# A different order of DMAs, additions, weight pieces and parameter steps in a kernel's opening

## The chip, the cores and the metric

One core of one Trainium2 chip runs the kernel, which is a single launch. The metric is the device time of one execution in microseconds (us). The kernel before takes 1205.55 us, the median of 3 runs from 1204.6 to 1206.71.

## What is computed

512 tokens (256 context tokens, then 256 latent ones) of width 1024 pass through two layers. The part of the reference that the opening of layer 0 computes, and the mixers whose preparation runs beside it:

```python
x = x + _pos_embed_2d(...)                    # latent tokens only: row part, column part
sh1, sc1, ... = split(silu(c) @ w_mod + b_mod) # c_ctx for the context tokens
h = x * rsqrt(mean(x * x) + EPS) * g * (1 + sc1) + sh1
z = h @ w_in                  # 5 * 256 mixer columns, 4 * 1024 gate columns
dt = exp(log_dt); mag = exp(lam_re * dt); ang = lam_im * dt      # S5 parameters
a_re, a_im = mag * cos(ang), mag * sin(ang)   # then f, b_bar, and a scan over the tokens
y = [s5(z0), fnet(z1), pool(z2), conv31(z3 * sigmoid(z4))]       # four branches
x = x + gate1 * ((sum of sigmoid(z_gate) * (y @ w_branch)) @ w_out)
```

## The kernel before

The activations lie transposed, with features on the partitions: `X[:, k, :]` is feature tile k (of 8) of all 512 tokens. A float32 product is made of three matmuls on a high and a low part of each factor (`tile_mm`, line 64 in the profile as for every recorded operation). The high and low parts of the normed input are `HH` and `HL`, in the tensor `parts`.

**Weights.** `Stream` brings 512 KB pieces in a fixed order on SyncE's (SP's) queue into three buffers. ScalarE (ACT) copies the high part, VectorE (DVE) subtracts it and so makes the low part: rows `TENSOR_TENSOR parts<-whole,parts 128x1024`, called a *low* below. `weight(j)` takes such a piece.

**Modulation.** `w_mod` comes in sixteen 512 KB pieces for the first half. `mod_part()` multiplies the next one (16 rows `bank<-..., 128*32 128x128` in the trace for a piece). Four pieces make one accumulated group, after which ACT copies it; `mod_finish(m)` then computes shift and scale of two feature tiles (m, m+1). `h_tiles` makes HH and HL of one tile per `next(h)`. `group(k, j)` is the three matmuls of feature tile k with weight j. In the opening, mod tiles 0 to 7 are wanted in pairs by the groups of k = 0 to 7. Four weights (j = 0 to 3) are multiplied in this way, 32 groups or 96 matmuls in all.

**Norm.** DVE and GpSimd (POOL) add the position tables to the latent half of X, ACT squares each tile, DVE adds the eight squares, and one set of four matmuls sums over features; `norm_steps` makes 1/rms of it.

**Warm matmuls.** `warm(n)` issues n products of 128x256 whose result nothing reads; there are 18 in the opening (7, then 2, 2, 0, 1, 2, 4).

**Background tasks.** The S5 parameters are computed by generators: `S5.prep` (small DVE operations, then complex powers), `tables_b` (48 DVE operations 128x256 that make 16 tables), `tables_c` (the same for the readout, on POOL, after a DMA from `s5c` at line 325), then a scan. `step(task, n)` advances one by n yields; in the opening it is called 3 times with 3, and once with 1. After the opening a planner (`pump`) puts the steps of all tasks between the matmuls by estimated engine times, so that a changed opening changes the order of everything that follows it in layer 0.

**After the opening** come the products of the weights in an order given by a string: z tiles 6, 8, 7, 9, then gate tiles (`g20`...), branch products (`q..`), and `y20`, `y10`: places where DVE splits a finished branch (FNet is y10) into high and low parts, which PE's next `q10` needs. In the trace these splits are rows `parts<-mixer,parts 128x512 x2`. The convolution needs z tile 9: its gate is a row `TENSOR_TENSOR scan<-scan,whole 128x512` (shown as 128x2x256 in the order rows); after it come 62 rows `SCALAR_TENSOR_TENSOR scan<-scan,whole 128x512`, two for each of 31 taps.

Of the kernel before, what the change touches and what calls it, by code (L numbers as in the profile page):

```python
# [104 lines left out]
class S5:  # L105
# [10 lines left out]
    def prep(self, tmp):  # L116
# [10 lines left out]
        K.nc.sync.dma_start(par, K.I["s5p"][self.l][:, 0:48])  # L127
        K.nc.sync.dma_start(raw, K.I["s5p"][self.l][:, 48:560])
# [608 lines left out]
class Model:  # L737
# [357 lines left out]
    def norm_steps(self, accs, n, width, d=None):  # L1095
# [3 lines left out]
        pss = [self.aux() for _ in accs]  # L1099
# [185 lines left out]
    def layer(self, l):  # L1285
# [10 lines left out]
        if l == 0:  # L1296
# [14 lines left out]
            parts(2)  # L1311
            self.warm(2)
            norm = self.norm_steps(((self.ACC,),), 512, 1024)
            next(norm)
            self.warm(2)
            parts(1)
            self.warm(0)
            parts(1)
            y = [y for y in norm][-1]
            self.warm(1)  # L1320
            self.mod_finish(0)
            self.warm(2)
# [5 lines left out]
            self.warm(4)  # L1328
            h = self.h_tiles(l, 0, r, 0, 512)
            weight(0)  # L1330
            next(h)
            next(h)
            group(0, 0)
            self.stream.advance(1)
            self.mod_ahead = 16
            parts(1)
            next(h)
            weight(1)
            parts(1)
            group(1, 0)  # L1340
            weight(2)
            parts(2)
            group(0, 1)
            self.mod_finish(2)
            next(h)
            next(h)
            group(1, 1)
            group(0, 2)
            group(1, 2)
            self.step(tab[0], 3)  # L1350
            group(2, 0, 1, 2)
            parts(1)
            weight(3)
            group(3, 0)
            parts(1)
            group(3, 1)
            parts(1)
            parts(1)
            group(3, 2)
            self.mod_finish(4)  # L1360
            next(h)
            next(h)
            group(0, 3)
            group(1, 3)
            group(2, 3)
            group(3, 3)
            self.step(tab[0], 3)
            group(4, 0, 1)
            parts(2)
            group(4, 2)  # L1370
            parts(2)
            group(4, 3)
            self.mod_finish(6)
            next(h)
            next(h)
            self.step(tab[0], 3)
            group(5, 0, 1, 2, 3)
            group(6, 0, 1, 2, 3)
            group(7, 0, 1, 2, 3)
        else:  # L1380
            gw = []

# [290 lines left out]
    def run(self):  # L1673
        nc = self.nc
# [462 lines left out]
```

## Time and profile before

| | us |
|---|---|
| median of 3 runs | 1205.55 |
| profiled execution, own time | 1209.18 |
| its span from first to last instruction | 1207.2 |
| PE busy in the span | 1160.9 (96%) |
| DVE busy | 976.1 (81%) |
| ACT busy | 517.1 (43%) |
| POOL busy | 282.9 (23%) |
| mean granted TensorE clock | 0.986 of full |

The profiled execution took 3.63 us more than the median, of which 1.98 us lie outside its span. A busy engine is one that holds an instruction; TensorE (PE) is busy nearly all of the time, so that time is to be had from its waits, from the stretches at a lower clock and from its work. Rows of the timeline give the start of a run of like instructions, its length, the engine, operation, tiles, shape and count, and in brackets the idle time ahead of it with what ended it. A start is counted from the span's start.

### The profile page before, as it was taken

The numbers are of one execution on the slowest core, as the hardware profiler recorded it, in microseconds if no ns is written. First come the engines' busy times: TensorE is split into PE (matmuls) and PEld (weight loads), VectorE is DVE, ScalarE is ACT, GpSimd is POOL, SyncE is SP. The second block draws the span as 40 slices with busy tenths as digits, with TensorE's granted clock in tenths as the row PEclk, the third lists the DMA queues.
The fourth block names the chain that finished last, engine by engine and source line by source line (L and its number), as shares of the span: only waits on it lengthen the run. The fifth ranks groups of instructions, "written<-read, shape, count | busy, mean of one in ns | idle before, by whom it ended". The sixth has DMA issues, their size and how long they took to land.

```text
span 1207.2 us, 20297 instructions
## 1 busy us (share of the span) xinstructions
PE 1160.9 (96%) x7770; PEld 1009.4 (84%) x7770; DVE 976.1 (81%) x1878; ACT 517.1 (43%) x872; POOL 282.9 (23%) x319
## 2 busy tenths in 40 slices
PE   7999897999999999999999899999899999999997
PEld 5777675777888988888887778898899999999997
DVE  6789989977999769999988883546998788867764
ACT  4534242344324365422332333346544556645543
POOL 0038656000000100166555561020520001000000
PEclk9999999999999999999999999999899999999999
DMA  9543531644674514466578774425554545555551
GB/s 366 225 144 109 180 92 52 229 156 138 212 229 156 173 37 148 140 188 230 186 245 296 249 247 180 130 98 177 173 166 167 159 160 205 177 190 179 189 182 48
DMA packets 66513, 211.49 MB, mean 175 GB/s; under 512 B 7984, under 2 KB 13616, under 8 KB 66416
## 3 DMA queue, kind: packets, MB, share of 16 engines
q1 hardware_dynamic: 55456, 183.84, 45.4%
q10 hardware_dynamic: 7696, 14.56, 3.3%
q0 software_dynamic: 3264, 11.80, 2.9%
q8 instruction: 61, 1.00, 0.3%
q14 instruction: 36, 0.29, 0.1%
HBM read 199.19 MB, written 10.98 MB: 174 GB/s over the span
## 4 chain that ended last, share of the span: by engine, by line
PE 72%; DVE 15%; POOL 3%; DMA 3%; issue 3%; ACT 3%; ACTq 0%; POOLq 0%; DVEq 0%; SPq 0%
PE bank L64 72%; DVE scan L64 5%; DVE parts L64 4%; DVE mixer L64 2%; DVE whole L64 2%; ACT parts L64 2%; POOL tables L64 1%; POOL whole L64 1%; ACT whole L64 1%; DVE windows L64 1%; POOL scan L64 1%; DMA whole<-in_w_in_dram 1%; DMA whole<-in_x_dram 0%; DMA scan<-scr_z 0%; DMA scr_c<-tables 0%
## 5 line engine op out<-in xcount | busy, mean ns | idle before, releaser
L64 PE MATMUL bank<-parts 128*128 128x512 f32 (+2 forms) x4008 | 727.2, 339 | 19.0 <-DVE parts L64 16.6
L64 PEld LDWEIGHTS bank<-parts 128*128 128x128 f32 x4008 | 616.3, 191 | 105.4 <-DVE parts L64 22.3
L64 ACT ACTIVATE parts<-whole 128x1024 fp32r<-128x1024 f32 (+1 forms) x288 | 273.7, 959 | 144.9 <-PE bank L64 73.9
L64 DVE TENSOR_TENSOR parts<-whole,parts 128x1024 fp32r<-128x1024 f32 (+1 forms) x240 | 294.0, 1233 | 16.0 <-ACT parts L64 15.6
L64 PE MATMUL bank<-hidden,parts 128*128 128x256 f32 (+1 forms) x1440 | 251.2, 335 | 0.0
L64 PEld LDWEIGHTS bank<-hidden,parts 128*128 128x128 f32 x1440 | 217.5, 188 | 29.9 <-issue 0.3
L64 DVE SCALAR_TENSOR_TENSOR whole<-whole 128x1024 f32<-128x1024 f32 (+4 forms) x188 | 175.7, 936 | 15.2 <-DMA whole<-in_w_modt_dram 12.0
L64 POOL TENSOR_TENSOR whole<-whole 128x256 f32<-128x256 f32 (+1 forms) x69 | 50.3, 743 | 347.2 <-ACT whole L64 342.2
L64 DVE SCALAR_TENSOR_TENSOR whole<-bank,whole 128x256 f32<-128x256 f32 (+1 forms) x121 | 54.7, 475 | 66.4 <-PE bank L64 66.2
L64 ACT ACTIVATE whole<-whole 128x256 f32<-128x256 f32 (+2 forms) x139 | 48.9, 388 | 107.2 <-DVE whole L64 96.4
L64 ACT ACTIVATE mixer<-bank 128x512 f32<-128x512 f32 (+1 forms) x84 | 40.7, 496 | 119.8 <-PE bank L64 110.3
L64 DVE TENSOR_TENSOR whole<-whole 128x256 f32<-128x256 f32 (+7 forms) x158 | 73.0, 467 | 16.7 <-ACT whole L64 11.7
L64 ACT ACTIVATE whole<-bank 128x512 f32<-128x512 f32 (+2 forms) x69 | 35.5, 537 | 109.1 <-PE bank L64 77.5
L64 POOL TENSOR_TENSOR tables<-tables,whole 128x256 f32<-128x256 f32 x48 | 61.4, 1287 | 37.4 <-DMA scr_c<-tables 34.9
L64 DVE TENSOR_TENSOR hidden<-whole,hidden 128x512 fp32r<-128x512 f32 (+2 forms) x77 | 53.4, 698 | 9.0 <-ACT hidden L64 2.4
L64 ACT ACTIVATE hidden<-whole 128x512 fp32r<-128x512 f32 (+2 forms) x77 | 47.1, 615 | 8.2 <-PE bank L64 2.3
L64 ACT ACTIVATE tables<-bank 128x512 f32<-128x512 f32 (+2 forms) x20 | 8.4, 422 | 92.8 <-PE bank L64 92.5
L64 POOL COPY whole<-whole 128x32 f32<-128x32 f32 x20 | 11.9, 626 | 150.3 <-DVE whole L64 150.3
L64 POOL TENSOR_TENSOR scan<-scan,whole 128x256 f32<-128x256 f32 (+3 forms) x50 | 44.0, 892 | 12.0 <-DVE scan L64 8.3
L64 DVE SCALAR_TENSOR_TENSOR scan<-scan,whole 128x512 f32<-128x512 f32 (+1 forms) x64 | 42.7, 728 | 0.0
L64 PE MATMUL bank<-merged,parts 128*128 128x256 f32 (+1 forms) x240 | 38.0, 316 | 0.8 <-DVE merged L64 0.8
L64 DVE TENSOR_TENSOR scan<-scan,whole 128x256 f32<-128x256 f32 (+5 forms) x61 | 31.5, 543 | 9.0 <-ACT whole L64 8.0
(115 smaller groups left out, 899.0 us busy)
## 6 DMA issues: line engine op xcount, KB each, us to landing
whole<-in_w_dram SPq DMA_DIRECT2D x128, 512.0 KB, 4.3
whole<-in_w_in_dram SPq DMA_DIRECT2D x84, 512.0 KB, 4.3
whole<-in_w_modt_dram SPq DMA_DIRECT2D x78, 512.0 KB, 4.1
whole<-in_w_br_dram SPq DMA_DIRECT2D x16, 512.0 KB, 4.4
whole<-in_w_out_dram SPq DMA_DIRECT2D x16, 512.0 KB, 4.2
mixer<-in_w_mod_dram SPq DMA_DIRECT2D x8, 512.0 KB, 9.7
scan<-scr_b POOLq DMA_DIRECT2D x8, 512.0 KB, 5.2
scan<-in_w_mod_dram SPq DMA_DIRECT2D x6, 512.0 KB, 9.7
```

The lines of the kernel that those rows point to most:

```text
L64: return f(out, *a, **k)
```

## The change

The S5 parameters' first load (48 columns) is issued first on SP's queue, ahead of X; the remaining 512 columns come after modulation piece 7, with a yield between the two. The first weight stands ahead of the modulation pieces. The two position tables become one DMA, first on ACT's queue, and DVE makes all eight additions. The squares are added in pairs on DVE, and PE sums the four pairs (16 matmuls of 128x1 in place of 4). Sigmoid runs after the first two squares and not before them. Thirteen of the 18 warm matmuls are gone. The steps of `prep` are called at 9 places (17 steps with the empty one) in place of 4 (10 steps). The groups and modulation pieces are multiplied in another order. The rows of `layer` that are taken out are in the listing above, and are shortened to a line of dots here.

```diff
--- before.py
+++ after.py
@@ -125,6 +125,7 @@
         par = A(48)
         raw = A(512)
         K.nc.sync.dma_start(par, K.I["s5p"][self.l][:, 0:48])
+        yield
         K.nc.sync.dma_start(raw, K.I["s5p"][self.l][:, 48:560])
         T = [A(16) for _ in range(12)]
         lr, li, dt = par[:, 0:16], par[:, 16:32], par[:, 32:48]
@@ -1092,11 +1093,11 @@
             self.nc.scalar.activation(t[:, sl], self.X[:, k, sl], AF.Square)
             self.defer(lambda: E.tensor_tensor(self.ACC[:, sl], self.ACC[:, sl], t[:, sl], op=ADD))
 
-    def norm_steps(self, accs, n, width, d=None):
+    def norm_steps(self, accs, n, width, d=None, pss=None):
         nc, V = self.nc, self.nc.vector
         self.settle()
         nt = n // 128
-        pss = [self.aux() for _ in accs]
+        pss = pss or [self.aux() for _ in accs]
         for ps, group in zip(pss, accs):
             for i in range(nt):
                 for a in group:
@@ -1308,73 +1309,72 @@
             def weight(j):
                 gw.append(self.stream.take(("in", l, gm[j])))
 
...
+            prep = tab[0]
+            weight(0)
+            norm = self.norm_steps((), 512, 1024, pss=[self.sums])
             y = [y for y in norm][-1]
...
+            parts(4)
             d, r = self.tmp(), self.aux()
             for i in range(4):
                 sl = slice(128 * i, 128 * i + 128)
                 nc.vector.tensor_scalar(d[:, sl], self.ident, y[:, i:i + 1], None, op0=MUL)
                 nc.tensor.matmul(r[:, sl], self.ones, d[:, sl], start=True, stop=True)
...
             h = self.h_tiles(l, 0, r, 0, 512)
...
+            next(h)
+            self.mod_finish(0)
+            self.warm(2)
+            next(h)
+            group(0, 0)
+            self.mod_ahead = 16
+            parts(1)
+            self.stream.advance(1)
+            next(h)
+            weight(1)
+            self.step(prep, 2)
+            group(1, 0)
+            parts(2)
+            group(0, 1)
+            group(1, 1)
+            parts(1)
+            self.step(prep, 2)
+            self.mod_finish(2)
+            next(h)
+            self.stream.advance(1)
+            group(2, 0, 1)
+            next(h)
+            parts(1)
+            weight(2)
+            self.step(prep, 2)
+            group(3, 0, 1)
+            parts(1)
+            group(0, 2)
+            group(1, 2)
+            parts(1)
+            self.stream.advance(1)
+            group(2, 2)
+            weight(3)
+            self.step(prep, 2)
+            group(3, 2)
+            parts(1)
+            group(0, 3)
+            self.mod_finish(4)
+            next(h)
+            group(1, 3)
+            group(2, 3)
+            next(h)
+            self.step(prep, 1)
+            group(3, 3)
+            parts(1)
+            group(4, 0, 1, 2, 3)
+            parts(2)
+            group(5, 0, 1)
+            parts(1)
+            self.step(prep, 2)
+            self.mod_finish(6)
+            group(5, 2, 3)
             next(h)
             next(h)
...
+            self.step(prep, 2)
             group(6, 0, 1, 2, 3)
             group(7, 0, 1, 2, 3)
         else:
@@ -1681,14 +1681,11 @@
                        + [b.base[:, b.lo + 1024 * i:b.lo + 1024 * i + 1024] for i in range(2)])
         cc = self.small[:, 0:16]
         mk = self.SCRA.mark()
-        prow, pcol = self.SCRA(16), self.SCRA(256)
+        pos = self.SCRA(272)
+        nc.scalar.dma_start(pos, I["pos"])
+        nc.scalar.dma_start(self.CONST[:, 0:264], I["const"][:, 0:264])
         nc.scalar.dma_start(cc, I["cc"])
-        nc.scalar.dma_start(prow, I["pos"][:, 0:16])
-        nc.scalar.dma_start(pcol, I["pos"][:, 16:272])
-        nc.scalar.dma_start(self.CONST[:, 0:264], I["const"][:, 0:264])
         nc.scalar.dma_start(self.PV[0][:, 0:142], I["pv"][0])
-        for k in range(0, 8, 2):
-            nc.sync.dma_start(self.X[:, k:k + 2, :], I["x"][:, k:k + 2, :])
         self.pre = [S5(self, 0), None]
         half = [self.A5.sub(3600), self.A5.sub(2400)]
         self.tab0 = []
@@ -1699,32 +1696,44 @@
             self.tab0.append(self.start(self.pre[0].tables_b(half[0], nc.vector), "d", 3.5))
 
         self.tab0.append(self.start(make0(), "d", 0.0))
-        self.mod_load()
-        while self.stream.load():
-            pass
-        self.step(self.tab0[0], 1)
-        self.mod_ahead = 8
-        self.mod_load()
+        prep = self.tab0[0]
+        self.step(prep, 1)
+        for k in range(0, 8, 2):
+            nc.sync.dma_start(self.X[:, k:k + 2, :], I["x"][:, k:k + 2, :])
+        for ahead in (4, 8, 10):
+            self.stream.load()
+            self.mod_ahead = ahead
+            self.mod_load()
+            if ahead == 8:
+                self.step(prep, 1)
         nc.vector.memset(self.CACT, 0.0)
-        self.warm(7)
+        self.step(prep, 2)
         t = self.tmp()
-        nc.scalar.activation(t[:, 0:16], cc, AF.Sigmoid)
-        nc.vector.tensor_tensor(self.CACT[:, :, 0:2], t[:, 0:16].rearrange("p (k c) -> p k c", c=2),
-                                cc.rearrange("p (k c) -> p k c", c=2), op=MUL)
-        pr = prow.rearrange("p (k r) -> p k r", k=4)
-        pc = pcol.rearrange("p (k r) -> p k r", k=4)
-        sq = []
+        pr = pos[:, 0:16].rearrange("p (k r) -> p k r", k=4)
+        pc = pos[:, 16:272].rearrange("p (k r) -> p k r", k=4)
+        self.warm(3)
+        self.sums = self.aux()
+        sq = [self.ACC if k == 0 else self.SIGR[k % 4] if k < 5 else self.TMP[k % 4] for k in range(8)]
+
+        def sums(k):
+            nc.vector.tensor_tensor(sq[k], sq[k], sq[k + 1], op=ADD)
+            for i in range(4):
+                nc.tensor.matmul(self.sums[:, i:i + 1], sq[k][:, 128 * i:128 * i + 128], self.ones[:, 0:1],
+                                 start=k == 0 and i == 0, stop=k == 6 and i == 3)
+
         for k in range(8):
             x = self.X[:, k, 256:512].rearrange("p (r c) -> p r c", r=4)
             pe = bc(pr[:, k, :, None], [128, 4, 64]) if k < 4 else bc(pc[:, k - 4, None, :], [128, 4, 64])
-            (nc.gpsimd if k in (1, 3, 5) else nc.vector).tensor_tensor(x, x, pe, op=ADD)
-            sq.append(self.ACC if k == 0 else self.SIGR[k % 4] if k < 5 else self.TMP[k % 4])
+            nc.vector.tensor_tensor(x, x, pe, op=ADD)
             nc.scalar.activation(sq[k], self.X[:, k, :], AF.Square)
-            if k in (3, 4):
-                nc.vector.tensor_tensor(sq[k - 3], sq[k - 3], sq[k - 1], op=ADD)
-        V = nc.vector.tensor_tensor
-        for i, j in ((1, 5), (0, 4), (0, 1), (0, 6), (0, 7)):
-            V(sq[i], sq[i], sq[j], op=ADD)
+            if k == 1:
+                nc.scalar.activation(t[:, 0:16], cc, AF.Sigmoid)
+            if k % 2 and k > 1:
+                sums(k - 3)
+            if k == 3:
+                nc.vector.tensor_tensor(self.CACT[:, :, 0:2], t[:, 0:16].rearrange("p (k c) -> p k c", c=2),
+                                        cc.rearrange("p (k c) -> p k c", c=2), op=MUL)
+        sums(6)
         self.SCRA.reset(mk)
         self.layer(0)
         self.area["left"].close()
```

On PE, the first rows with a `parts` operand are the groups. Rows `bank_70<-` are modulation pieces (x8 for each piece), banks 64, 65, 66 and 63 are those of weights j = 0, 1, 2, 3, and `128x8` is the first instruction of a `mod_finish`. Before, from the first group:

```order
L64 MATMUL bank_64<-parts 128x512 x3
L64 MATMUL bank_70<-mixer,whole 32x128 x8
L64 MATMUL bank_70<-scan,whole 32x128 x8
L64 MATMUL bank_64<-parts 128x512 x3
L64 MATMUL bank_70<-scan,whole 32x128 x16
L64 MATMUL bank_65<-parts 128x512 x3
L64 MATMUL bank_68<-whole 128x8
L64 MATMUL bank_65<-parts 128x512 x3
```

and after the change:

```order
L64 MATMUL bank_64<-parts 128x512 x3
L64 MATMUL bank_70<-mixer,whole 32x128 x8
L64 MATMUL bank_64<-parts 128x512 x3
L64 MATMUL bank_70<-scan,whole 32x128 x16
L64 MATMUL bank_65<-parts 128x512 x6
L64 MATMUL bank_70<-scan,whole 32x128 x8
L64 MATMUL bank_68<-whole 128x8
```

The eighth modulation piece now stands behind both groups of weight 1, and the second `mod_finish` behind it; before, one group of weight 1 stood ahead of that.

On DVE, around the convolution's gate (the row `scan<-scan,whole 128x2x256`; for weight z9 it is the second one). Rows `whole<-whole 128x16x2` and the like are the powers at the end of `prep`, `mixer<-` rows are pooling windows. Before:

```order
L64 TENSOR_TENSOR parts<-whole,parts 128x1024 x2
L64 MEMSET scan 128x2x15 x2
L64 TENSOR_TENSOR scan<-scan,whole 128x2x256
L64 TENSOR_TENSOR scan<-whole 128x32 x2
L64 TENSOR_TENSOR whole<-whole 128x16x2 x2
L64 TENSOR_TENSOR whole<-whole,scan 128x16x2 x2
L64 TENSOR_TENSOR scan<-whole 128x64 x2
L64 TENSOR_TENSOR whole<-whole 128x16x4 x2
L64 TENSOR_TENSOR whole<-whole,scan 128x16x4 x2
L64 TENSOR_TENSOR parts<-whole,parts 128x1024
L64 TENSOR_TENSOR mixer<-mixer,whole 64x2x256 x2
L64 TENSOR_TENSOR mixer<-mixer 128x2x256
```

and after the change:

```order
L64 TENSOR_TENSOR whole<-whole,scan 128x16x4 x2
L64 TENSOR_TENSOR parts<-whole,parts 128x1024 x2
L64 TENSOR_TENSOR mixer<-mixer 128x2x258
L64 TENSOR_TENSOR mixer<-mixer 64x2x256
L64 TENSOR_TENSOR scan<-scan,whole 128x2x256
L64 TENSOR_TENSOR mixer<-mixer,whole 64x2x256 x2
L64 TENSOR_TENSOR mixer<-mixer 128x2x256
L64 TENSOR_TENSOR parts<-whole,parts 128x1024 x2
L64 MEMSET scan 128x2x15 x2
L64 TENSOR_TENSOR scan<-scan,whole 128x2x256
L64 TENSOR_TENSOR mixer<-mixer 128x2x270
L64 TENSOR_TENSOR mixer<-mixer 128x2x268
```

The powers, a low, and the first pooling window's three rows now stand ahead of the second gate.

On SP's queue, the loads from `s5c` that POOL's `tables_c` waits for. Before, in the stretch behind the opening's last modulation piece:

```order
L684 DMA whole<-in_w_in_dram 128x1024 x8
L684 DMA whole<-in_w_br_dram 128x1024
L684 DMA whole<-in_w_in_dram 128x1024 x2
L325 DMA scan<-in_s5c_dram 128x128 x2
L684 DMA whole<-in_w_in_dram 128x1024 x2
```

and after the change:

```order
L685 DMA whole<-in_w_in_dram 128x1024 x8
L326 DMA scan<-in_s5c_dram 128x128 x2
L685 DMA whole<-in_w_br_dram 128x1024
L685 DMA whole<-in_w_in_dram 128x1024 x2
L326 DMA scan<-in_s5c_dram 128x128
```

They stand three weight loads earlier.

## Rows read from the trace of the kernel before

**Rows 1.** PE's waits in the whole span: total us, times, longest

```profile
PE bank L64 <- DVE parts L64: 16.6, 10, 7.8
PE bank L64 <- POOL scan L64: 3.9, 2, 2.1
PE bank L64 <- DMA scan<-scr_z: 2.2, 1, 2.2
PE bank L64 <- DVE scan L64: 1.6, 2, 1.0
```

**Rows 2.** Timeline of PE, around its longest wait

```profile
189.14 14.43 PE L64 MATMUL bank<-parts 128*128 128x512 f32 x61
211.41 4.88 PE L64 MATMUL bank<-parts 128*128 128x512 f32 x12 [7.84 <-DVE parts L64]
```

**Rows 3.** Busy time by stretch: us, PE, PEld, DVE, ACT, POOL, clock, DMA share, GB/s

```profile
0.00:50.00 50.00, 42.42 (x391) 30.99 (x392) 32.19 (x90) 22.96 (x42) 2.49 (x7) 1.00 0.76 297
90.00:140.00 50.00, 44.41 (x287) 33.45 (x288) 48.84 (x66) 21.03 (x46) 37.48 (x49) 0.93 0.36 127
93.00:94.00 1.00, 1.00 (x3) 0.77 (x3) 1.00 (x3) 0.95 (x5) 0.92 (x2) 0.50 0.65 256
140.00:200.00 60.00, 57.77 (x347) 46.02 (x347) 54.46 (x118) 21.94 (x66) 36.62 (x43) 0.97 0.32 103
```

**Rows 4.** Timeline of PE in the opening

```profile
22.54 0.50 PE L64 MATMUL bank<-parts 128*128 128x512 f32 x1 [0.51 <-ACT parts L64]
38.44 4.35 PE L64 MATMUL bank<-parts 128*128 128x512 f32 x18
46.57 13.63 PE L64 MATMUL bank<-parts 128*128 128x512 f32 x59
```

**Rows 5.** Timeline of ACT in the opening

```profile
3.13 1.28 ACT L64 ACT_TABLE_LOAD   x1 [3.13 <-issue]
21.39 1.09 ACT L64 ACTIVATE parts<-whole 128x256 fp32r<-128x256 f32 x2 [2.45 <-DVE whole L64]
```

**Rows 6.** Timeline of DVE, 28 to 160 us

```profile
28.87 0.17 DVE L64 TENSOR_TENSOR whole<-bank,whole 128x8 f32<-128x8 f32 x1 [0.58 <-PE bank L64]
77.41 0.69 DVE L64 TENSOR_TENSOR scan<-scan,whole 128x512 f32<-128x512 f32 x1 [3.51 <-ACT whole L64]
82.31 2.20 DVE L64 TENSOR_TENSOR mixer<-mixer 128x512 f32<-128x512 f32 x3
90.54 0.85 DVE L64 TENSOR_TENSOR scan<-whole 128x256 f32<-128x256 f32 x1
106.91 0.86 DVE L64 TENSOR_TENSOR whole<-whole 128x256 f32<-128x256 f32 x1
123.92 0.42 DVE L64 TENSOR_TENSOR whole<-whole 128x256 f32<-128x256 f32 x1
134.60 3.39 DVE L64 SCALAR_TENSOR_TENSOR scan<-scan,whole 128x512 f32<-128x512 f32 x5
158.69 1.22 DVE L64 TENSOR_TENSOR parts<-whole,parts 128x1024 fp32r<-128x1024 f32 x1 [4.75 <-ACT parts L64]
```

**Rows 7.** Timeline of POOL, 80 to 160 us

```profile
84.97 0.77 POOL L64 TENSOR_SCALAR scan<-scan 128x64 f32<-128x64 f32 x1 [1.38 <-DMA scan<-in_s5c_dram]
133.14 0.80 POOL L64 TENSOR_TENSOR scan<-scan,whole 128x256 f32<-128x256 f32 x1
145.08 9.11 POOL L64 TENSOR_TENSOR whole<-whole 128x16 f32<-128x16 f32 x15
```

**Rows 8.** DVE's groups by shape, 90.5 to 133.3 us: count, busy us, mean ns

```profile
L64 DVE TENSOR_TENSOR scan<-whole 128x256 f32<-128x256 f32 x16 | 12.5, 782 | 0.0
L64 DVE TENSOR_TENSOR whole<-whole 128x256 f32<-128x256 f32 x16 | 12.3, 769 | 0.6 <-POOL scan L64 0.6
L64 DVE TENSOR_TENSOR scan<-scan,whole 128x256 f32<-128x256 f32 x16 | 11.3, 707 | 0.5
```

More of the change, by code (lines that the diff above doesn't have):

```diff
@@ L1309, in weight @@
                 gw.append(self.stream.take(("in", l, gm[j])))
[L1311 to L1318, printed above, removed]
+            prep = tab[0]
+            weight(0)
+            norm = self.norm_steps((), 512, 1024, pss=[self.sums])
             y = [y for y in norm][-1]
-            self.warm(1)
-            self.mod_finish(0)
-            self.warm(2)
+            parts(4)
             d, r = self.tmp(), self.aux()
@@ L1327, in layer @@
                 nc.tensor.matmul(r[:, sl], self.ones, d[:, sl], start=True, stop=True)
-            self.warm(4)
             h = self.h_tiles(l, 0, r, 0, 512)
-            weight(0)
+            next(h)
[10 more added lines that the diff above has]
+            group(1, 0)
@@ L1331, in layer @@
+            group(5, 2, 3)
             next(h)
             next(h)
[L1333 to L1377, printed above, removed]
+            self.step(prep, 2)
             group(6, 0, 1, 2, 3)
```

## Prediction

> **What bounds the kernel now.** I read the page first (PE holds an instruction for 96% of the span), then the list of PE's waits, then the timeline around each. All named waits together are a few tens of us, and the largest single one is 7.8 us [rows 1]. It stands where PE has finished what it has (189.14 + 14.43 = 203.57) and waits until 211.41 for DVE's split of the FNet branch, y10 [rows 2]. To that split DVE runs almost without a gap: it is busy 48.84 of 50 us from 90 to 140 and 54.46 of 60 from 140 to 200 [rows 3]. So there are two regimes: in the opening (to about 55 us) PE follows DVE, ACT and the DMAs, and from 90 to 211 us DVE's queue decides when PE may go on. The change touches the opening, and through it DVE's order up to 211. From 211.41 on, the profiled execution has 1207.2 - 211.41 = 995.8 us left, nearly all of it PE's work, and I let that stand. The profiled execution is 1209.18, the median 1205.55; I apply the difference to the median.
>
> **The opening, part by part.** Removing 13 of 18 warm matmuls is free as far as they lie in PE's idle time. Three additions that come from POOL cost DVE about 3 × 0.4, and four fewer additions of squares give it back; I set both at nothing, for DVE is busy 32.19 of the first 50 us [rows 3].
>
> Sigmoid now stands after a square, so there are two table loads on ACT and not one. Here the row shows 1.28 us for one [rows 5]; the second stands between squares, and the norm waits for the last of them. I take 1.28 as its price on the norm, in sum with the norm's other shortenings (sums on PE, low of weight 0 ahead of it): the first high part of h, at 21.39 before [rows 5], comes at about 19.7 (estimated between 18.5 and 21), and the first group about 1.7 us earlier than 22.54 [rows 4]. The Trainium skill, "ScalarE: Activation LUTs", section "What ACT_TABLE_LOAD costs", states a load of about 1283 ns and a drain of about 1380 ns, 2.66 us for a switch. By it the first group would be only 0.3 us earlier; the row agrees with the load, and the drain is not a row here.
>
> That lead is not kept. The next gate is the second `mod_finish` (DVE's row at 28.87 [rows 6]), which needs the eighth modulation piece. The change puts both groups of weight 1 ahead of that piece, and these need a high and a low part of h and the second weight's low, with four steps of `prep` between; I estimate it at the same 29 us. But by then two groups fewer have been multiplied than before. A group's three matmuls take 3 × 4.35/18 = 0.73 us at this place [rows 4], so that is 1.4 us. The order afterwards alternates each group with a modulation piece or a weight's low; I add 0.8 us for one more wait for a low part that is 1.22 long [rows 6]. Before, the opening's last 36 matmuls ended at 46.57 + 36 × 13.63/59 = 54.9 [rows 4]. I take 57.0 (+2.2); bounds 53.5 (the 1.7 us are kept) and 58 (two more such waits).
>
> **DVE's ledger to the split.** The z tiles 6, 8, 7, 9 are 96 matmuls at 0.23, 22 us; so z9 ends at 78.9 (76.8 before), and the convolution's gate on DVE starts at 79.5, where it was at 77.41 [rows 6]. Before, 13.1 us passed from there to the first operation of `tables_b` at 90.54 [rows 6]. Of these, the powers, one low and the first part of the pooling windows now stand ahead of the gate, in DVE's wait of 3.51 us and earlier idle time (the six additional `prep` steps have moved into the opening). Behind it stay the gate itself (0.6) and what ran from 82.31 to 90.54 but one of its first three rows (8.23 - 0.73 = 7.5) [rows 6]: first `tables_b` operation at 79.5 + 8.1 = 87.6, and 88.0 with POOL busy beside it. That is **-2.5**. Bounds: -6 with an opening of 53.5, -1.5 with 58.
>
> From there to the split the order lists the same work but for two more convolution taps (0.68 each, 3.39 for 5 [rows 6]) and one more low (1.2): **+2.5**.
>
> The 48 operations of `tables_b` took 36.1 us in all [rows 8]. One takes 0.42 us when POOL waits and 0.86 when POOL works [rows 6]. POOL's `tables_c` began at 84.97, released by its `s5c` load [rows 7]; that is 5.6 us ahead of `tables_b`. The load now stands three weight loads earlier and the powers are ready earlier, so I estimate the start at 76, 12 us ahead. Some 6.5 us of POOL's work then no longer run beside `tables_b`, worth 6.5 × (1 - 0.42/0.86) = 3.3 us if nothing slides back; POOL has waits of its own in between that may. I take **-2.0**, bounds 0 and -3.3.
>
> Later DVE stood 4.75 us until 158.69 for a high part on ACT [rows 6], which stood behind POOL's fifteen small products (145.08 to 154.19 [rows 7]). These need `tables_b` to be done, 4.5 us earlier by the terms so far, so they end at 149.7 and that high part is ready 4.5 us later, at 154.2. DVE comes there at 153.9 - 4.5 + 2.5 = 151.9, and would wait 2.3 us. If POOL's end is another 2 us earlier, because it is done with `tables_c` well before 133.94 [rows 7], the wait is nearly gone. I take **-3.2** (bounds -2.4 and -4.7).
>
> Sum: -2.5 + 2.5 - 2.0 - 3.2 = **-5.2**, so PE goes on at 206.2 in place of 211.4.
>
> **PE's own arrival there.** From 54.9 to 203.57 lie 148.7 us. Of these 7.7 are waits [rows 1], and a mean clock of 0.93 over 50 us and 0.97 over 60 means 7 + 3.6 us at the lower level of 1.2 GHz (0.50 as at 93 [rows 3]), which cost half of that, 5.3. PE's work is then 135.7, and from 57.0 on it arrives at 192.7 plus its waits: with as many as before, at 205.7. That is just under 206.2, so the two meet; the long wait of 7.8 us should all but vanish, and 5.2 us are gained at most times. **Forecast: 1205.55 - 5.2 = 1200.3.**
>
> **Rivals.**
>
> *PE becomes the limit.* The order puts the products of the tables and the transposes of the scan at places estimated from another opening; the y20 split moves behind more of `tables_b`. With 3.5 us more of waits or of the lower clock PE arrives at 209.2, and the change brings 2.2 us: 1203.4. For it speaks that PE would come only 0.5 us ahead of the split; against it that part of the waits ends with POOL's `tables_c`, which is earlier. This counts as no change.
>
> *The opening runs at the lower clock.* Before, the granted clock was 1.00 through the first 50 us [rows 3], with warm matmuls between. Now PE stands still in the norm, and the groups that follow are in pieces. After a wait of 2 us at 90 the clock was at 1.2 GHz and cost 1.8 us or so of the 5.3. Two such stretches in the opening cost 3.5 us and move everything by as much, less DVE's spare time: 1202 to 1204. The Trainium skill, "TensorE: Matmul & The Clock Gate", section "Part 1: The HAM clock gate", says that an idle TensorE is brought to the lower rate; the trace agrees in that the clock fell after 90 us to 0.50.
>
> *Slower: POOL runs beside all of `tables_b`.* If `tables_c` starts no earlier or pauses so that it lies wholly beside `tables_b`, each of the 48 operations takes 0.86: 41.3 us, 5.2 more than 36.1. With it -2.5 + 2.5 + 5.2 - 2.4 = +2.8 and the POOL block at 145 is no earlier (+1.5): +4.3, 1209.9. It decides the sign from a mean of about 0.83 us per operation, where before it was 0.75. For it: DVE and POOL already overlap for 37.48 of 50 us. Against: the earlier `s5c` load.
>
> *The opening is shorter after all.* The 1.7 us lead is kept and the 13 warm matmuls' places are used: the opening ends at 53.5, `tables_b` begins 3.5 us earlier than in my sum, of which DVE's queue keeps most: 1196.5 to 1197.
>
> **How the numbers follow.** Two runs of this kernel agree to about 0.2%, 2.4 us, so that is the bound for no change: 1203.1 to 1207.9. Chances: forecast 0.45 (its own range 1197.5 to 1203), shorter opening 0.12, PE as limit 0.20, lower clock 0.08, POOL beside all 0.15. Faster: nearly all of the first two, and a few hundredths of the next two, 0.59. Slower: the last, 0.15, with some for orders beyond 211 us that I let stand (the modulation of later pieces moves too, up to 3 us either way): 0.18. No change: 0.23. The range runs from the shorter opening with half of the idle bounds, 1195, to the POOL rival, 1209.
>
> **What would show it.** In the changed profile: the first row `bank<-parts` at about 20.9 us and two ACT_TABLE_LOAD rows; the opening's last matmuls at about 57; POOL's first TENSOR_SCALAR of `tables_c` at about 76 and DVE's first 128x256 product at 88; the mean of those 48 near 0.70; the split y10 at about 205.5, and PE's wait there under 3 us. I am wrong if the opening does not end between 53.5 and 58, if POOL's start stays at 85, if those means are above 0.8, or if after 212 us a wait appears that was not there.

## The result

The changed kernel is slower: 1215.22 us (median of 4 runs, 1212.98 to 1216.42) beside 1206.05 for the kernel before on the same chip, ratio 1.0075, 95% interval 1.0058 to 1.0093. The prediction was 1200.3, in a range from 1195 to 1209. Chips differ, and the kernel before had medians of 1206 to 1211 on the four used, so each kernel below is read by its ratio to the kernel before on its own chip.

The profiled execution of the changed kernel took 1215.1 with a span of 1213.3, near its median; that of before lay 3 us above its median, so the two traces show 5.9 of the 9.2 us.

PE in the opening of the changed kernel, in the columns of the earlier timelines (a row joins neighbours with the same tiles and shows the shape of the first, so that the x14 are the eight rows of the products for 1/rms, two of a `mod_finish` and four of warm matmuls):

```profile
17.47 2.79 PE L64 MATMUL bank<-mixer,whole 128*32 128x128 f32 x48
20.19 3.33 PE L64 MATMUL bank<-whole 128*128 128x128 f32 x14
24.45 0.50 PE L64 MATMUL bank<-parts 128*128 128x512 f32 x1 [0.92 <-ACT parts L64]
32.29 0.39 PE L64 MATMUL bank<-whole 128*128 128x8 f32 x2 [0.40 <-ACT whole L64]
34.26 0.50 PE L64 MATMUL bank<-parts 128*128 128x512 f32 x1 [1.58 <-ACT parts L64]
46.05 0.28 PE L64 MATMUL bank<-whole 128*128 128x8 f32 x2
55.62 0.39 PE L64 MATMUL bank<-whole 128*128 128x8 f32 x2 [0.40 <-ACT whole L64]
58.66 11.40 PE L64 MATMUL bank<-parts 128*128 128x512 f32 x49 [0.56 <-DVE parts L64]
```

The first group is at 24.45, 1.9 later than [rows 4]. The last 23 of the 96 group matmuls lie in the last row, so that the opening ends at 58.66 + 23 × 11.40/49 = 64.0: 9.1 later than before, where I had +2.2. PE and DVE behind it:

```profile
87.73 1.00 DVE L64 TENSOR_TENSOR scan<-scan,whole 128x512 f32<-128x512 f32 x1 [4.03 <-ACT whole L64]
97.52 0.97 DVE L64 TENSOR_TENSOR scan<-whole 128x256 f32<-128x256 f32 x1
213.09 1.29 DVE L64 TENSOR_TENSOR parts<-mixer,parts 128x512 fp32r<-128x512 f32 x2
```

```profile
213.83 12.44 PE L64 MATMUL bank<-parts 128*128 128x512 f32 x47 [5.06 <-DVE parts L64]
229.63 2.19 PE L64 MATMUL bank<-scan 128*32 128x128 f32 x80 [3.36 <-ACT scan L64]
434.63 1.21 PE L64 MATMUL bank<-parts 128*128 128x256 f32 x8 [0.68 <-DVE parts L64]
```

The convolution's gate is 10.3 late against [rows 6], the first table product 7.0, PE's restart at the FNet split only 2.4 [rows 2]. So DVE's queue gave back most of the opening's loss, as the prediction's ledger says it can. Then comes a wait that was not there: 3.36 us for ACT, with the 80 readout products now 47 matmuls behind the split. The products behind layer 0's second norm are at 434.63. In the trace of before the readout stood 68 matmuls behind the split and did not wait:

```profile
211.41 17.58 PE L64 MATMUL bank<-parts 128*128 128x512 f32 x68 [7.84 <-DVE parts L64]
228.94 1.75 PE L64 MATMUL bank<-scan 128*32 128x128 f32 x80
427.14 1.22 PE L64 MATMUL bank<-parts 128*128 128x256 f32 x8 [0.67 <-DVE parts L64]
```

At the second norm this is +7.5: 2.4 of the restart, 3.36 of the new wait, and most of the rest from the lower clock after it (the 80 rows take 2.19 us in place of 1.75, and the 18 behind them 5.47 in place of 4.39). Two questions follow: what lengthened the opening, and what became of the time that DVE's queue gave back.

### The profile page after: what moved, and what is told of

Same layout as the page of the kernel before. It is cut to its first block, busy times and chain, and to the rows that moved or that the text cites. A ratio compares the mean times of both kernels' runs of the same rounds, so it can differ in the third digit from the quotient of the medians.

```text
span 1213.3 us, 20272 instructions
## 1 busy us (share of the span) xinstructions
PE 1158.4 (95%) x7768; PEld 1004.8 (83%) x7768; DVE 973.9 (80%) x1878; ACT 518.4 (43%) x873; POOL 276.2 (23%) x316
## 4 chain that ended last, share of the span: by engine, by line
PE 54%; DVE 26%; issue 6%; DMA 6%; POOL 4%; ACT 4%; ACTq 0%; DVEq 0%; SPq 0%; POOLq 0%
PE bank L64 54%; DVE whole L64 9%; DVE parts L64 7%; DVE scan L64 4%; DVE mixer L64 3%; POOL tables L64 2%; POOL whole L64 2%; ACT parts L64 2%; ACT whole L64 1%; DMA whole<-in_w_in_dram 1%; DMA whole<-in_w_dram 1%; DVE tables L64 1%; DMA scr_c<-tables 1%; DVE windows L64 1%; DVE hidden L64 1%
## 5 line engine op out<-in xcount | busy, mean ns | idle before, releaser
L64 DVE TENSOR_TENSOR parts<-whole,parts 128x1024 fp32r<-128x1024 f32 (+1 forms) x240 | 295.4, 1238 | 10.6 <-ACT parts L64 10.3
L64 DVE SCALAR_TENSOR_TENSOR whole<-whole 128x1024 f32<-128x1024 f32 (+3 forms) x186 | 174.0, 936 | 16.0 <-DMA whole<-in_w_modt_dram 9.4
L64 ACT ACTIVATE mixer<-bank 128x512 f32<-128x512 f32 (+1 forms) x84 | 40.8, 497 | 128.1 <-PE bank L64 121.0
L64 DVE TENSOR_TENSOR whole<-whole 128x256 f32<-128x256 f32 (+7 forms) x157 | 69.9, 452 | 16.4 <-ACT whole L64 10.8
L64 DVE TENSOR_TENSOR mixer<-mixer 128x512 f32<-128x512 f32 (+11 forms) x60 | 35.9, 603 | 5.3 <-ACT mixer L64 4.6
## 6 DMA issues: line engine op xcount, KB each, us to landing
scan<-in_w_mod_dram SPq DMA_DIRECT2D x6, 512.0 KB, 10.3
```

The lines of the kernel that those rows point to most:

```text
L64: return f(out, *a, **k)
```

## The experiments

The table gives each kernel's ratio with its interval and, from its trace, the first group, the opening's end (worked out as above), the FNet split on DVE and the products behind the second norm on PE (all us). Five of them issue the same instructions up to the first group (changed, after_head_old_tail, late_readout, swap, hyb_late), and there it stands at 23.10 to 24.45. So a difference of up to 1.35 us between two traces at this place shows nothing by itself.

| kernel | ratio | interval | first group | opening ends | split | second norm |
|---|---|---|---|---|---|---|
| before | 1 | | 22.54 | 54.9 | 210.67 | 427.14 |
| changed | 1.0075 | 1.0058 to 1.0093 | 24.45 | 64.0 | 213.09 | 434.63 |
| old_layer | 1.0062 | 1.0042 to 1.0083 | 28.11 | 60.4 | 208.20 | 434.63 |
| old_run | 1.0079 | 1.0048 to 1.0111 | 26.34 | 66.8 | 211.48 | 435.23 |
| prep_only | 1.0025 | 1.0002 to 1.0048 | 23.22 | 55.6 | 208.81 | 428.70 |
| one_table | 1.0097 | 1.0075 to 1.0120 | 23.57 | 63.6 | 212.35 | 434.81 |
| after_head_old_tail | 1.0018 | 1.0001 to 1.0034 | 24.31 | 56.8 | 206.11 | 427.60 |
| more_warm | 1.0068 | 1.0045 to 1.0092 | 29.43 | 69.5 | 218.45 | 437.42 |
| late_readout | 1.0023 | 0.9998 to 1.0047 | 23.96 | 64.8 | 213.56 | 433.02 |
| swap | 1.0064 | 1.0041 to 1.0088 | 23.10 | 61.2 | 209.96 | 432.12 |
| hyb_late | 0.9960 | 0.9941 to 0.9980 | 23.79 | 56.2 | 205.61 | 422.75 |
| hyb_late_one | 0.9956 | 0.9938 to 0.9973 | 22.26 | 54.9 | 204.40 | 422.58 |
| prep_late | 0.9968 | 0.9949 to 0.9987 | 22.99 | 55.4 | 208.54 | 425.79 |
| before_late | 1.0017 | 0.9996 to 1.0037 | 26.73 | 59.0 | 214.84 | 434.25 |

**old_layer**: the layer's opening taken from before, all else as changed. Against the opening of before, one line differs:

```diff
             parts(2)
             self.warm(2)
-            norm = self.norm_steps(((self.ACC,),), 512, 1024)
+            norm = self.norm_steps((), 512, 1024, pss=[self.sums])
```

> The changed kernel, but with the layer's order of groups, modulation pieces and warm matmuls as before; the loads, the additions, the sums of squares and the two table loads stay as changed. Theory A (the loss arises in the order of groups and pieces in the layer: PE has nothing to multiply while the second pair of h tiles is made): the first group starts at 23 to 24.5 us, the opening ends at 56 to 58 us in place of 64.0, and the median is 1204 to 1209. Theory B (the loss arises ahead of the first group: later x, two table loads, TensorE at the lower clock from 12 to 22 us): the opening still ends at 61 us or later and the median is 1212 or more.

Neither came about as stated. From the first group (28.11) to the end (60.4) it takes 32.3 us, as before (32.4), in place of 39.5; so the order of groups is guilty of 7 us. But the first group itself came 5.6 us late. Two things stand in PE's rows, and this run does not part them: the 11 warm matmuls and four pieces of the old order queue behind 16 matmuls of sums, and the sums run at the lower level (eight rows 128x1 take 1.86 us at 9.28, 1.05 in the changed kernel). And with a split earlier than before (208.20) PE does not wait at the split but elsewhere, and why there was not tested:

```profile
226.43 15.49 PE L64 MATMUL bank<-parts 128*128 128x512 f32 x60 [5.78 <-DVE mixer L64]
```

**old_run**: loads, additions, squares and first warm matmuls from before, the layer's opening as changed.

```diff
-            norm = self.norm_steps((), 512, 1024, pss=[self.sums])
+            norm = self.norm_steps(((self.ACC,),), 512, 1024)
```

> The changed kernel, but with the loads, additions, squares, Sigmoid and first warm matmuls as before; only the layer's order of groups and pieces and the place of the prep steps in it are as changed. Theory A (the layer's order loses the time): first group at 22 to 23 us, opening ends at 60 to 63 us, median 1210 to 1214. Theory B (the time is lost ahead of the first group): opening ends at 54 to 57 us, median 1207 or less.

From first group to end 40.5 us: the changed order loses about the same with either head. Its wait at the second gate (the second `mod_finish`) is the same as well:

```profile
37.06 0.50 PE L64 MATMUL bank<-parts 128*128 128x512 f32 x1 [1.58 <-ACT parts L64]
```

Theory B's forecast failed. The first group at 26.34 does not fit theory A either: PE stood 5.66 us before the sums, and its clock was at 0.50 from 15 to 26 us.

**after_head_old_tail**: the changed head, and from the first group on the order of before with 4, 4 and 5 prep steps.

```diff
             group(0, 0)
-            self.mod_ahead = 16
-            parts(1)
-            self.stream.advance(1)
...
+            self.stream.advance(1)
+            self.mod_ahead = 16
+            parts(1)
...
+            self.step(prep, 4)
```

> The changed kernel up to its first group, and from there the order of groups, modulation pieces and weights of before, with 4, 4 and 5 prep steps where before had 3 each. Theory A (from the first group on, the changed order costs some 7 us: two groups of weight 1 and more stand ahead of the last pieces that a mod_finish needs, and nothing is left to multiply while h tiles are made): the first group stays at 24.4 us, the opening ends at 56 to 58 us in place of 64.0, and the convolution's gate is at 79 to 81 in place of 87.7; the median falls to 1207 to 1211. Theory B (a lead in the opening is used up by DVE's queue before 211 us): the opening ends at 56 to 58, but PE goes on after the FNet split at most 2 us earlier than 213.8 and the median stays at 1213 or more.

This is theory A's result: opening at 56.8, 7.2 us earlier than the changed kernel, and a ratio of 1.0018. In the trace PE still has groups left at the gate that feeds the second pair of h tiles:

```profile
30.33 0.29 PE L64 MATMUL bank<-whole 128*128 128x8 f32 x2
33.26 2.11 PE L64 MATMUL bank<-parts 128*128 128x512 f32 x8 [0.27 <-DVE parts L64]
```

0.27 us of wait in place of 1.58 and 0.56. And it is the opening of 57 us that my ledger assumed. The split comes at 206.11, where I had 205.5 on DVE; but the lead is given back at the readout:

```profile
206.84 13.64 PE L64 MATMUL bank<-parts 128*128 128x512 f32 x47 [4.66 <-DVE parts L64]
222.72 2.93 PE L64 MATMUL bank<-scan 128*32 128x128 f32 x80 [2.24 <-ACT scan L64]
427.60 1.21 PE L64 MATMUL bank<-parts 128*128 128x256 f32 x8 [0.67 <-DVE parts L64]
```

4.6 us ahead at the restart, 0.5 behind at the second norm.

**swap**: one exchange in the changed order.

```diff
+            parts(1)
             group(0, 1)
-            group(1, 1)
-            parts(1)
             self.step(prep, 2)
             self.mod_finish(2)
             next(h)
+            group(1, 1)
             self.stream.advance(1)
```

> The changed kernel with one exchange: the eighth modulation piece and the second mod_finish stand ahead of the second groups of weight 1, one of which covers the making of the h tiles. If PE's lack of a cover is what makes the second gate late: mod_finish 0.9 to 1.7 us earlier than 32.3, the wait of 1.58 us for the high part shrinks to 0.8 or less, the opening ends 1.5 to 2.5 us earlier than 64.0, and the median falls by 1 to 2.5. Rival (the gate waits for the piece's landing or DVE): nothing earlier by more than 0.5 us.

The wait for the high part is halved (0.79 us in place of 1.58), and from first group to end it takes 38.1 in place of 39.5 (39.5 to 40.8 in the five other traces with the changed order). The effect is there and small, and PE still waits 0.56 for the low part and 0.40 and 0.56 around the fourth gate. The ratio shows no difference; PE's restart is 3.1 us earlier than the changed kernel's (210.69), and the wait at the readout 3.73 us.

**prep_only**: the kernel before with the early parameters and 4 prep steps at each of the three places.

```diff
         K.nc.sync.dma_start(par, K.I["s5p"][self.l][:, 0:48])
+        yield
         K.nc.sync.dma_start(raw, K.I["s5p"][self.l][:, 48:560])
...
-            self.step(tab[0], 3)
+            self.step(tab[0], 4)
```

> The kernel before, with one part of the change alone: the 48 columns of recurrence parameters loaded ahead of x, the 512 later, and 12 + 4 prep steps within the opening in place of 9 + 1. If early parameter steps are worth what the prediction gave them (the table operations begin about 2.5 us earlier than 90.5 us, and the wait before the FNet split shrinks): median 1200 to 1203.5. If the time saved is taken up by DVE's other work or by contention with POOL: 1204 to 1208. If DVE work in the opening delays h tiles or lows: the opening ends later than 55.5 us and the median is above 1208.

By its numbers the run lies on the edge of the third case (opening's end 55.6, where 55.5 was the bound, ratio 1.0025). The trace speaks for the second, that the time is taken up: the split is earlier, and the lead is gone behind it. POOL's `tables_c` begins 10.7 us earlier than [rows 7], while the first table product on DVE does not move (90.54 before [rows 6]):

```profile
74.24 0.69 POOL L64 TENSOR_SCALAR scan<-scan 128x64 f32<-128x64 f32 x1 [2.84 <-DMA scan<-in_s5c_dram]
```

```profile
90.19 0.86 DVE L64 TENSOR_TENSOR scan<-whole 128x256 f32<-128x256 f32 x1
```

The split is 1.9 us earlier, and there is a new wait at the readout, as in the changed kernel:

```profile
225.45 1.75 PE L64 MATMUL bank<-scan 128*32 128x128 f32 x80 [2.79 <-ACT scan L64]
```

**late_readout**: the changed kernel with one number of the planner, the estimated time in us that it leaves between the readout's loads and its products.

```diff
                 self.window((h,), raw)
-                yield "w", 10.0
+                yield "w", 16.0
```

> The changed kernel with one number of the planner changed: the readout's products are put 16 us of estimated time behind their window loads, in place of 10. Theory (the new wait of 3.36 us at 229.6 us is a placement by the planner, which puts the 80 products 47 matmuls behind the FNet split where before it put 68): the wait vanishes, with its stretch at the lower clock, and the median falls by 3 to 5 us, to 1210 to 1212. Rival: PE waits as long for the next of DVE's results, and the median stays within 1.5 us of 1215.

The wait is gone: 74 matmuls follow the split without a gap.

```profile
214.29 18.75 PE L64 MATMUL bank<-parts 128*128 128x512 f32 x74 [4.36 <-DVE parts L64]
```

The ratio falls from 1.0075 to 1.0023, on another chip, though in its trace, which lies 4.6 us above its median, only 1.6 us are gained at the second norm.

**hyb_late, prep_late, before_late**: the same number in after_head_old_tail, in prep_only and in the kernel before.

> The changed kernel's head with the order of before from the first group on, and with the readout's products 16 us of estimated time behind their window loads in place of 10. Theory (with the opening at 57 us the FNet split comes 4.6 us earlier than before, and that lead was given back to the readout's wait of 2.24 us and its lower clock): no wait for ACT near 222 us, the products behind the second norm (at 427.1 us before) start at 422 to 425 us, and the ratio to before is 0.994 to 0.998. Rival (the lead is used up wherever DVE's queue decides, also in layer 1): they start at 426 us or later, or the lead is lost behind 600 us, and the ratio is 1.000 to 1.003.

> The kernel before with the early recurrence parameters and prep steps alone, and the readout's products 16 us behind their window loads. Theory: the wait of 2.79 us at 225 us that the early parameters had caused vanishes, the products behind the second norm start at 424 to 426 us in place of 428.7, and the ratio to before is 0.996 to 0.999. Rival (early parameters are worth nothing in the end): ratio 1.000 to 1.003.

> The kernel before with the readout's products 16 us of estimated time behind their window loads in place of 10: the control. The kernel before has no wait there, so the theory expects a ratio of 0.998 to 1.002; if it falls below 0.998, the later place is a gain by itself and none of the early opening.

The theory holds in all three. hyb_late is faster than before, 0.9960 with an interval below 1:

```profile
206.34 19.38 PE L64 MATMUL bank<-parts 128*128 128x512 f32 x74 [4.33 <-DVE parts L64]
225.65 1.75 PE L64 MATMUL bank<-scan 128*32 128x128 f32 x80
422.75 1.22 PE L64 MATMUL bank<-parts 128*128 128x256 f32 x8 [0.68 <-DVE parts L64]
```

The 4.4 us of lead at the second norm against before are most of what the restart had won (206.34 against 211.41, 5.1). The later place by itself is no gain: the control stands at 1.0017.

Two things follow that the single runs don't say. Four kernels make a table of two by two: the changed head with either order of groups and either number, each read against before on its own chip. The old order brings 0.0057 with 10.0 and 0.0063 with 16.0, the later readout 0.0052 with the changed order and 0.0058 with the old one. So the two losses add up, each some 6 to 8 us, and with both repaired the changed head measures 0.9960, where the forecast was 1200.3/1205.55 = 0.9956. But prep_late, with the later readout and nothing of the change but the early parameters and steps, stands at 0.9968, and the two intervals overlap: nothing shows that the other parts of the changed head (additions on DVE, sums on PE, fewer warm matmuls) gain anything.

**more_warm**: ten more warm matmuls in the changed kernel.

```diff
                 sums(k - 3)
+                self.warm(2)
...
             parts(4)
+            self.warm(4)
```

> The changed kernel with ten more warm matmuls: two after each of the first three sums of squares, four after the four modulation pieces. If the lower clock at 12.6 to 22.4 us is due to PE's gaps and counts: granted clock 1.00 there, first group 1.5 to 3 us earlier than 24.45, median lower by up to as much. If the clock counts for little, since DVE and ACT set the first group: first group at most 0.7 us earlier. If the warm matmuls stand in the way of the sums: first group later.

The third case: the first group comes 5 us later. In PE's queue the warm matmuls stand ahead of the sums and of the products for the norm:

```profile
16.15 1.71 PE L64 MATMUL bank<-whole,mixer 128*128 128x1 f32 x8
17.72 4.56 PE L64 MATMUL bank<-whole 128*128 128x256 f32 x28
24.37 3.97 PE L64 MATMUL bank<-whole 128*128 128x256 f32 x22
```

Yet the ratio, 1.0068, is no higher than the changed kernel's. Its trace is 5.5 us later at the opening's end, 5.4 at the split and 2.8 at the second norm, for the wait at the readout is down to 0.85 us. A late opening is not paid in full at the end.

**one_table** and **hyb_late_one**: Sigmoid ahead of the squares and its input first on ACT's queue, in the changed kernel and in hyb_late.

```diff
+        nc.scalar.activation(t[:, 0:16], cc, AF.Sigmoid)
...
-            if k == 1:
-                nc.scalar.activation(t[:, 0:16], cc, AF.Sigmoid)
```

> The changed kernel with Sigmoid ahead of all squares, and its input loaded first on ACT's queue, so that ACT loads one table set. Theory B (time lost ahead of the first group counts in full): the first group starts 1.3 to 2.7 us earlier than 24.45 and the median falls by as much, to 1212.5 to 1214. Theory A: the first group starts earlier, but the second pair of h tiles is made no more than 0.5 us earlier, and the median stays at 1214 to 1216.

> The kernel of the run above with Sigmoid ahead of all squares and its input first on ACT's queue: one table load in place of two. If the second table load counts once the groups follow in the old order: the first group 0.7 to 1.3 us earlier than 24.3, the opening's end as much earlier, and the ratio lower by 0.0005 to 0.001 than in the run above. If it is hidden: no difference.

The first group is 0.9 and 1.5 us earlier, which is near the 1.28 of the load's row, but 23.57 lies within the 23.10 to 24.45 of the five heads with two loads, and only 22.26 below them. In the changed kernel the second gate gains 0.4 us of that and the ratio nothing (1.0097; the intervals overlap). In hyb_late_one the opening ends 1.3 us earlier and the second norm 0.2: 0.9956 beside 0.9960, no difference that these runs can tell. So a price of the second table load on the first group is likely but not shown, and nothing of it can be seen in the end.

## Why the prediction was wrong

**What bounds the kernel** was right up to the split: the long wait there, and DVE's queue from 90 to 211 us that ends it.

**The step that failed first is the opening's end, 57.0 for 64.0.** It has two terms of equal size, 3.6 and 3.4 us. The first group was forecast 1.7 us earlier and came 1.9 later. I had counted the sums on PE among the norm's shortenings and the moved pieces at nothing (and four fewer additions of squares on DVE, where it is three, seven before and four now). The rows show both on the path: the four sums of pairs and four pieces occupy PE until 20.19, so that the four products for 1/rms start only there, when DVE had already made all four of their operands (19.98), and DVE waits for them:

```profile
19.11 0.87 DVE L64 TENSOR_SCALAR whole<-whole 128x128 f32<-128x128 f32 x4
22.31 0.69 DVE L64 TENSOR_TENSOR whole<-whole,bank 128x512 f32<-128x512 f32 x1 [2.32 <-PE bank L64]
```

The lower clock is another part of it. swap issues the same instructions up to here, and its PE was back at the upper level from 20 us on:

```profile
19.77 2.25 PE L64 MATMUL bank<-whole 128*128 128x128 f32 x14
```

The 14 rows that took 3.33 us from 20.19 take 2.25 from 19.77, and the first group comes at 23.10, 1.35 earlier. So 1.35 of the 3.6 us went with the clock of this one execution. The rest was there in swap too, with the sums at the lower level in all five heads.

more_warm shows that a longer queue of PE at this place goes into the first group. ACT's first table load also waits for x at 6.01, where before it stood at 3.13 [rows 5] beside loads:

```profile
6.01 1.28 ACT L64 ACT_TABLE_LOAD   x1 [6.01 <-DMA whole<-in_x_dram]
...
8.47 1.28 ACT L64 ACT_TABLE_LOAD   x1
9.77 0.22 ACT L64 ACTIVATE whole<-whole 128x16 f32<-128x16 f32 x1
```

The second load costs 1.28 plus 0.02 until the next instruction. The Trainium skill ("ScalarE: Activation LUTs", section "What ACT_TABLE_LOAD costs") gives 2.66 us for a switch of tables, a load of about 1.28 and a drain of about 1.38. The load agrees; the drain doesn't show in these rows.

From the first group on I allowed 36.1 us and it took 39.5. I had counted the lead of 1.7 as lost at the second gate, two groups fewer (1.4) and one wait of 0.8; the mechanism is the one I named (the eighth piece behind both groups of weight 1), but I priced it at the one gate. The changed order leaves PE without ready groups behind the second and the fourth `mod_finish`. At the second one PE waits 1.58 + 0.56 us, its clock then falls, and the next gates are late by more each time: 3.7 us at 32.29, 7.8 at 46.05, 9.2 at 55.62. The gates of before:

```profile
28.55 0.28 PE L64 MATMUL bank<-whole 128*128 128x8 f32 x2
31.48 2.11 PE L64 MATMUL bank<-parts 128*128 128x512 f32 x8 [0.27 <-DVE parts L64]
38.30 0.28 PE L64 MATMUL bank<-whole 128*128 128x8 f32 x2
46.43 0.28 PE L64 MATMUL bank<-whole 128*128 128x8 f32 x2
```

The largest part lies between the second and the third gate. Both kernels multiply 27 group matmuls and four pieces there, before in 9.8 us and the changed kernel in 13.8. Of these 4.0 us 1.9 are the waits for h (1.58 + 0.56 for 0.27), and much of the rest is the lower level around 37 us. after_head_old_tail, old_layer and old_run agree on 7 to 8 us for the order, its waits and the clock behind them together.

**The clock**, a rival with 0.08, did appear in the opening:

```profile
14.00:22.00 8.00, 8.00 (x85) 7.38 (x86) 4.07 (x17) 0.49 (x2) 0.00 (x0) 0.50 1.03 419
36.00:39.00 3.00, 3.00 (x22) 1.80 (x21) 2.32 (x6) 2.13 (x4) 0.00 (x0) 0.52 0.17 66
140.00:200.00 60.00, 58.87 (x360) 47.10 (x358) 57.49 (x122) 23.47 (x68) 26.37 (x32) 1.00 0.31 101
```

From 14 to 22 us PE is at the 1.2 GHz level (0.50), and again around 37. Beyond the 1.35 us by which swap differs, how much of the first group's delay is the clock's and how much the longer queue's stays open: no execution of the changed head ran at the upper level throughout. On the other hand 90 to 200 us lost no clock, where before had lost 5.3 us by [rows 3].

**DVE's ledger was right in its later terms and short in its first, and its sum came out in part by luck.** The 48 table operations took 33.2 us (36.1 before [rows 8]), -2.9 for -2.0:

```profile
L64 DVE TENSOR_TENSOR scan<-whole 128x256 f32<-128x256 f32 x16 | 11.8, 740 | 0.0
L64 DVE TENSOR_TENSOR whole<-whole 128x256 f32<-128x256 f32 x16 | 11.1, 695 | 0.0
L64 DVE TENSOR_TENSOR scan<-scan,whole 128x256 f32<-128x256 f32 x16 | 10.3, 646 | 0.5
```

DVE's idle time from 140 to 200 fell from 5.5 [rows 3] to 2.5, -3.0 for -3.2. In after_head_old_tail, with the opening where I had put it, POOL's `tables_c` starts at 75.64 (76 forecast), and the split is at 206.11 (205.5). But the first table product is at 90.96, where I had 88.0:

```profile
81.15 1.00 DVE L64 TENSOR_TENSOR scan<-scan,whole 128x512 f32<-128x512 f32 x1 [4.01 <-ACT whole L64]
90.96 0.96 DVE L64 TENSOR_TENSOR scan<-whole 128x256 f32<-128x256 f32 x1
```

The term of -2.5 is +0.4 there: the gate comes 1.7 us later than its 79.5, and behind it 9.8 us pass, where I had 8.5. From the first table product to the split 115.2 us pass against 117.5 in the forecast, which pays back most of those 3.0.

The wait at the split, which I had at under 3 us, stayed at 5.06. PE needed 144.8 us from the opening's end until it stood there (190.26 + 18.51 - 64.0), where I had let the 148.7 of before stand; its clock was at 1.00 from 90 to 200 us.

**The step that failed second is that the 995.8 us behind the restart were let stand.** From restart to the span's end the changed kernel takes 1213.3 - 213.83 = 999.5, after_head_old_tail 1211.8 - 206.84 = 1005.0, hyb_late 1202.8 - 206.34 = 996.5. I had named a new wait behind 212 us as a sign that I was wrong, but given orders behind 211 us only 3 us either way. With the better opening alone, the readout's wait and others ate the whole gain (1.0018); with the later readout most of it is kept (0.9960), so that wait is shown as the main one. One wait for POOL's tables in layer 1 is among them: 8.6 us in after_head_old_tail where before had 4.2, in the list of waits.

```profile
PE bank L64 <- POOL tables L64: 8.6, 7, 1.6
```

That these waits in layer 1 come from the shifted plan is argued, not tested; hyb_late has 5.4 there.

So the miss adds up in the two traces: the restart at 213.83 for 206.2 is 7.6 us of it, what lies behind it 3.7. Most of the remaining 3.6 of the 14.9 between 1200.3 and 1215.22 comes from the forecast's starting point: the profiled execution of before lay 3.63 above its median, that of the changed kernel at its median.

**The other rivals.** POOL beside all of `tables_b`, the one on the slower side, did not happen (mean 0.69 us per operation, 0.75 before). PE as the limit did not either: it still waited 5.06 us at the split. The slower result came by a path that had no rival of its own: an opening beyond my bound of 58 us, and a wait behind the split.

## What to carry to other kernels

When pieces and products are interleaved by hand, look at each gate for what PE still has in stock while the gate's result is made, and price an exchange at every gate that follows the same pattern, not only at the first. Work moved to an idle engine in a serial stretch counts as soon as it stands in that engine's queue ahead of the critical product. And where a planner places later work by estimates, a time saved ahead of it may be kept only if what it places follows: here one number, six microseconds of estimated distance, turned 1.0018 into 0.9960, and was worth nothing in the kernel before.

## What the runs showed of the hardware that was not expected

The same opening instructions ran at two speeds. In before_late, whose opening is that of before instruction for instruction, the first modulation piece was multiplied at 12.30 (11.68 before), after a wait of 2.67 us in place of 0.89, PE was at the lower clock from 12 us on, and the first group came at 26.73 in place of 22.54:

```profile
12.30 1.08 PE L64 MATMUL bank<-whole 128*32 128x128 f32 x16 [2.67 <-DMA whole<-in_w_mod_dram]
26.73 0.49 PE L64 MATMUL bank<-parts 128*128 128x512 f32 x1 [0.51 <-ACT parts L64]
```

```profile
16.00:20.00 4.00, 4.00 (x18) 3.08 (x20) 1.63 (x10) 0.00 (x0) 0.00 (x0) 0.50 1.04 415
```

A later landing of 0.6 us thus went with 4.2 us in the opening. This is as large as what the experiments sought, and a reason to read ratios over many executions and not single traces.

The clock's record also misses a stretch at the start. In hyb_late eight rows 128x1 take 1.87 us at 9.33, in the changed kernel 1.05 at 9.23, and both show 1.00 from 8 to 10 us:

```profile
9.33 1.87 PE L64 MATMUL bank<-whole 128*128 128x1 f32 x8 [0.32 <-DVE whole L64]
```

```profile
9.23 1.05 PE L64 MATMUL bank<-whole 128*128 128x1 f32 x8 [0.32 <-DVE whole L64]
```

In such a stretch the durations of equal instructions, not the record, tell the level.
